# Scan drain, weight ring and FFN token sums of a hybrid encoder layer rearranged

## The chip, the cores and the metric

The kernel runs on one core of one Trainium2 chip. The metric is the device time of one execution in microseconds (us). The engines are TensorE (PE in the profile; PEld is its weight load), VectorE (DVE), ScalarE (ACT), GpSimd (POOL) and SyncE (SP), which issues the DMAs. Each engine takes its instructions in order; they meet through semaphores.

## The reference

One layer of an encoder over 1024 tokens of width 1024, in float32:

```
hn = rms_norm(x); u = hn @ w_in
y_a = MLA attention(u) @ w_br_mla      # 8 heads
y_b = forgetting attention(u) @ w_br_fox   # 8 heads
y_c = rms_norm((ssd_scan(...) + D * xh) * silu(z)) @ w_br_ssm
merged = g0 * y_a + g1 * y_b + g2 * y_c    # g = sigmoid(u_gate + b)
x = x + merged @ w_out
a = causal_dwconv(rms_norm(x) @ ffn_w_up) # 2 x 2816 columns, 3 taps
x = x + (silu(a_gate) * a_val) @ ffn_w_down
```

The scan carries a state of 16 heads, 64 by 128, from chunk to chunk; inside a chunk it is a masked product with exponentials of cumulated decays.

## The kernel before

**Products.** Every float32 product is made of three matmuls: each operand is split in a high part (rounded to the matmul's type by an ACT copy) and a low part (the rest, a DVE subtraction), and high x high, high x low and low x high are added in PSUM. `split` (L131) is the pair of instructions, `mm3` (L156) the loop. A matmul here is 128x128 by 128x512 as a rule.

**Order.** In the stages that matter PE's order is that of the program (`manual_schedule`); the instructions of the other engines are placed by a scheduler which simulates a timeline, except those wrapped in `pin`, which keep their program order. Tiles come from pools; a tag with `bufs` n is a ring of n buffers, and a tile that is laid over an older one, in its ring or in a closed pool, waits for that one's readers.

**The scan.** After the attention comes the scan over 8 chunks of 128 tokens, written as three generators. `ssd_a` transposes a chunk's inputs, forms the decay sums (`pse`, L1143, one PSUM bank with tag "seg") and their exponentials E; `ssd_b` (a chunk later) updates the state and forms the outputs (`py`, L1177, two banks with tag "py"), multiplies by the gate and scales each token by a reciprocal root (`rsqrt`, L140, all DVE, L1205 to L1208); `ssd_c` (a chunk later again) transposes the outputs (`stp`, L1216) and stores them to ys_d. `merge` interleaves these on PE with `fill`, a generator of independent projection matmuls (`all_fill`, L774; its matmuls are L791), by the share of its cost that each stream has done. Ten steps run; FILL_SSD (L1024) is how much of fill each step asks for, in units in which three matmuls are 0.65. What fill has left when the steps end is done afterwards.

**The merge and w_out.** Three branch products (`ybr`) run over 8 column tiles j and two token halves; the last branch adds up `merged[j]` and splits it to `mh`, `ml` (L1285, L1286). Then the pool of the early stages closes, a new one (`fill2`, L1290) opens in its place, w_out is loaded and split to `oh`, `ol` (L1373 to L1386), and `wo` runs over eight token tiles t and two column halves nh. `norm2` (L1302) normalises tile t-1 and transposes it (`pt`) into h2h, h2l; for the later half of the tokens it forms combinations instead, one of them T3f.

**The FFN's first matrix.** It is multiplied by a scheme with fewer products: seven block products per pair of column tiles instead of eight, with sums of weight blocks (S12, S34, `sums`, L1430) and of token blocks (T1 to T4). `prepare` (L1455) makes T3, T2 and T4 out of T3f on DVE and ACT, within the first pair. The first FIRST = 3 pairs have two of their products put ahead (`a_`, L1420). Each pair then needs products b0, c0, d0, sums X, Y, a convolution of three taps (`fa`, L1522 to L1525), silu and a product, and is stored to act_d.

**The FFN's second matrix.** It also runs as seven products (`steps`, L1536), 11 k-steps each, `dn` (L1624). The first EARLY = 3 loads use the FFN's rings; the rest use the pool "dr", which opens after "sk" (L1582, L1583).

Of the kernel before, what the change touches and what calls it, by code (L numbers as in the profile page):

```python
# [21 lines left out]
P = 128  # L22
D = 1024
# [19 lines left out]
def block_kernel(ctx: ExitStack, tc: tile.TileContext, x, positions, norm_mix_g, w_in, b_gate,  # L43
# [87 lines left out]
    def split(h, l, src, he=None, le=None):  # L131
        he = he or A
        le = le or V
        if he is A:
            A.activation(h, src, AF.Copy)  # L135
        else:
            he.tensor_copy(h, src)
        le.tensor_sub(l, src, f32(h))  # L138

    def rsqrt(pool, y, v, n):  # L140
# [6 lines left out]
        for _ in range(3):  # L147
# [6 lines left out]
            V.scalar_tensor_tensor(out=y, in0=t, scalar=1.5, in1=y, op0=ALU.add, op1=ALU.mult)  # L154

# [868 lines left out]
    FILL_SSD = [12.6] * 8 + [13.0, 13.0]  # L1024
# [45 lines left out]
    with ExitStack() as ps__:  # L1070
# [37 lines left out]
        def ssd_a(o, c):  # L1108
# [33 lines left out]
            for q in range(4):  # L1142
                pse = psp.tile([P, 512], F32, name=uid("pse"), tag="seg", bufs=1)  # L1143
# [13 lines left out]
        def ssd_b(o, c, prev):  # L1157
# [18 lines left out]
            def outputs(q):  # L1176
                py = psp.tile([P, 4, P], F32, name=uid("py"), tag="py", bufs=2)  # L1177
# [27 lines left out]
            V.tensor_scalar(v, ss, 1.0 / D, EPS, op0=ALU.mult, op1=ALU.add)  # L1205
            r = pool.tile([P, 1], F32, name=uid("yr1"), tag="yr1")
            rsqrt(pool, r, v, 1)
# [37 lines left out]
    with ExitStack() as pe_:  # L1245
        mp_ = pe_.enter_context(TP("mgp", 1))
        psp = pe_.enter_context(TP("pse", 6, space=PSUM))
        merged = [mp_.tile([P, S], F32, name=f"mg{j}", tag=f"mg{j}") for j in range(NK)]
# [4 lines left out]
        for b, wsrc, nk in ((1, w_br_fox, 4), (0, w_br_mla, 4), (2, w_br_ssm, 8)):  # L1253
# [15 lines left out]
            for j in range(NK):  # L1269
# [3 lines left out]
                for half in range(2):  # L1273
# [9 lines left out]
                    if b == 2:  # L1283
                        V.tensor_add(m, m, g[:, hs])
                        A.activation(mh[half][:, j, :], m, AF.Copy, scale=0.5)  # L1285
                        V.scalar_tensor_tensor(out=ml[half][:, j, :], in0=m, scalar=0.5,  # L1286
                                               in1=f32(mh[half][:, j, :]), op0=ALU.mult, op1=ALU.subtract)
    psg.close()
    pfl.close()
    fpl = ctx.enter_context(TP("fill2", 2, side="right"))  # L1290
# [6 lines left out]
    t3p = pt3.enter_context(TP("t3p", 1))  # L1297
    T3f = t3p.tile([P, 4, 512], F32, name="T3f", tag="T3f")
# [3 lines left out]
    def norm2(t, xt):  # L1302
        xn = fpl.tile([P, D], F32, name=uid("xn"), tag="t4", bufs=3)
# [20 lines left out]
        if half == 1:  # L1324
            b12 = xrp.tile([P, 4, P], F32, name=uid("b12"), tag="b12", bufs=2)
            A.activation(b12, pts[0], AF.Copy)
            V.tensor_sub(T3f[:, :, cs], pts[1], b12)
            e = V if t >= NT - 2 else G
            e.tensor_sub(b12, b12, f32(h2h[0][:, 0:4, cs]))
            e.tensor_sub(b12, b12, f32(h2l[0][:, 0:4, cs]))  # L1330
            hs = h2h[1][:, 0:4, cs]
            A.activation(hs, b12, AF.Copy)
            V.tensor_sub(h2l[1][:, 0:4, cs], b12, f32(hs))
# [11 lines left out]
    def halves(raw, n=NK):  # L1345
        tag, pool, bufs = ("wh", "wl"), fpl, 3
        if n == 4:
            tag, pool, bufs = ("h22", "l22"), upb, 1
        h = pool.tile([P, n, P], F32R, name=uid(tag[0]), tag=tag[0], bufs=bufs)
        l = pool.tile([P, n, P], F32R, name=uid(tag[1]), tag=tag[1], bufs=bufs)  # L1350
        split(h, l, raw)
        return h, l
# [13 lines left out]
    FIRST = 3  # L1366
# [3 lines left out]
    op_ = po_.enter_context(TP("op", 1))  # L1370
    wov = w_out[0].rearrange("(k p) c -> p k c", p=P)
    oh, ol = [], []
    for nh in range(2):  # L1373
        h = op_.tile([P, NK, 512], F32R, name=uid("woh"), tag=f"woh{nh}")
        l = op_.tile([P, NK, 512], F32R, name=uid("wol"), tag=f"wol{nh}")
        for k in range(0, NK, 2):
            late = nh == 0 and k >= 4
            raw = fpl.tile([P, 2, 512], F32, name=uid("raw"), tag="t4" if late else "wr", bufs=3 if late else 2)
            SY.dma_start(raw, wov[:, k:k + 2, 512 * nh:512 * nh + 512])
            if nh == 0:  # L1380
                for i in range(2):
# [295 lines left out]
```

## Time and profile before

| | us |
|---|---|
| median of three runs | 2154.65 |
| lowest and highest of them | 2147.74, 2155.8 |
| the profiled execution's own time | 2151.87 |
| its span | 2150.1 |
| w_out's first to last matmul | 1382.6 to 1481.8 |
| FFN first matrix, from its first product | 1483.7 to 1932.3 |
| FFN second matrix | 1932.1 to 2146.4 |

The profile shows one execution. A view of waits gives, for an engine, the line whose instruction waited, what ended the wait, and then the total, the number and the longest. A window gives the length of a stretch, the busy time of PE, PEld, DVE, ACT and POOL in it with their instructions, then the granted clock of PE as a share of full speed, the share of the DMA engines and their GB/s. A timeline row gives start, length, engine, line, operation, out<-in and shapes, and in brackets the idle time before it with its releaser. A group row ends with the total and mean (ns) of an instruction, then the idle time ahead of them. Matmuls overlap, so the mean of one is longer than their spacing.

### The profile page before, as it was taken

Reading aid. Unit: us, or ns where it says so; the run is one execution under the profiler, and the core shown is the slowest. Engines: PE = TensorE matmul, PEld = TensorE weight load, DVE = VectorE, ACT = ScalarE, POOL = GpSimd, SP = SyncE. Lnnn points to the kernel's source line nnn. Section 1 sums busy time; section 2 is a strip of 40 time slices with the busy share of each in tenths; the row PEclk is TensorE's granted clock in tenths of the full one; section 3 lists DMA queues with packets and bytes.
Section 4 is the critical chain, followed back from the end, with each engine's and each line's share of the span. In section 5 each row is a group of like instructions: output and inputs, shape, how many; then the busy total and the mean of one; then the engine's idle time right before and its main releaser. Section 6 shows DMA issues by size and latency. Waiting matters only on the chain. (4 is left out here: it accounts for less than half of the span.)

```text
span 2150.1 us, 29015 instructions
## 1 busy us (share of the span) xinstructions
PE 2056.7 (96%) x10221; PEld 1689.0 (79%) x10221; DVE 1414.1 (66%) x2574; ACT 948.2 (44%) x1701; POOL 669.9 (31%) x626
## 2 busy tenths in 40 slices
PE   7999899999999999999999799999899999999999
PEld 6898687778888888887777688777678888887887
DVE  6686478356766666657887356457887777665655
ACT  5554222145555555545555223223444444444432
POOL 2453123222222222222110030003454554431855
PEclk9999999999999999999999899999999999999999
DMA  5167667654344355424342565241122222239665
GB/s 169 36 190 217 235 208 231 207 153 127 108 135 123 104 136 137 110 76 130 109 129 94 167 200 186 98 147 50 59 88 79 79 89 79 79 111 321 239 210 196
DMA packets 275608, 303.07 MB, mean 141 GB/s; under 512 B 19292, under 2 KB 208744, under 8 KB 275464
## 3 DMA queue, kind: packets, MB, share of 16 engines
q1 hardware_dynamic: 275464, 301.24, 45.3%
q8 instruction: 80, 1.31, 0.3%
q14 instruction: 64, 0.52, 0.1%
HBM read 208.51 MB, written 92.67 MB: 140 GB/s over the span
## 5 line engine op out<-in xcount | busy, mean ns | idle before, releaser
L791 PE MATMUL mm<-hnh,wh 128*128 128x512 f32 x576 | 241.1, 419 | 1.6 <-ACT wh L741 1.6
L931 POOL TENSOR_SCALAR pm<-pm,rs 128x128 f32<-128x128 f32 (+7 forms) x128 | 108.5, 851 | 403.8 <-DVE rs L930 268.1
L791 PE MATMUL mm<-hnh,wl 128*128 128x512 f32 x576 | 228.6, 397 | 0.5 <-DVE wl L742 0.5
L791 PE MATMUL mm<-hnl,wh 128*128 128x512 f32 x576 | 228.1, 396 | 0.0
L1624 PE MATMUL dn<-dr,dr 128*128 128x512 f32 x616 | 190.8, 391 | 0.8 <-DVE dr L138 0.8
L924 ACT ACTIVATE pm<-s,nmx 128x128 f32<-128x128 f32 (+2 forms) x192 | 110.4, 580 | 71.1 <-DVE nmx L921 57.0
L1624 PEld LDWEIGHTS dn<-dr,dr 128*128 128x128 f32 x616 | 116.3, 189 | 25.1 <-DVE dr L138 1.1
L791 PEld LDWEIGHTS mm<-hnh,wl 128*128 128x128 f32 x576 | 109.1, 189 | 26.2 <-DVE wl L742 1.0
L791 PEld LDWEIGHTS mm<-hnh,wh 128*128 128x128 f32 x576 | 110.1, 191 | 20.9 <-issue 2.9
L791 PEld LDWEIGHTS mm<-hnl,wh 128*128 128x128 f32 x576 | 109.7, 190 | 17.0 <-issue 0.2
L905 PE MATMUL s<-qk,qk 96*128 96x384 f32 (+5 forms) x480 | 119.0, 352 | 3.4 <-DMA qk<-q_h 2.0
L1624 PE MATMUL dn<-dr 128*128 128x512 f32 x308 | 120.5, 391 | 1.8 <-ACT dr L135 1.8
L991 DVE TENSOR_TENSOR ptl<-tp,pth 128x512 fp32r<-128x512 f32 (+1 forms) x160 | 98.7, 632 | 29.9 <-ACT pth L990 28.9
L138 DVE TENSOR_TENSOR dr<-dr,dr 128x1024 fp32r<-128x1024 f32 x55 | 77.2, 1405 | 56.1 <-ACT dr L135 52.0
L162 PE MATMUL fx<-w5h,hnh 128*128 128x512 f32 x256 | 102.2, 404 | 7.7 <-ACT w5h L135 7.7
L135 ACT ACTIVATE wh<-wr 128x1024 fp32r<-128x1024 f32 (+1 forms) x46 | 41.9, 910 | 153.1 <-PE ybr L162 70.3
L990 ACT ACTIVATE pth<-tp 128x512 fp32r<-128x512 f32 (+1 forms) x160 | 84.1, 555 | 43.5 <-PE tp L985 43.1
L162 PE MATMUL ybr<-ah,wh 128*128 128x512 f32 x256 | 101.1, 400 | 1.6 <-ACT ah L135 1.6
L162 PE MATMUL fx<-w5h,hnl 128*128 128x512 f32 x256 | 102.3, 401 | 0.0
L162 PE MATMUL fx<-w5l,hnh 128*128 128x512 f32 x256 | 101.2, 397 | 0.0
L162 PE MATMUL ybr<-al,wh 128*128 128x512 f32 x256 | 100.9, 396 | 0.0
L162 PE MATMUL ybr<-ah,wl 128*128 128x512 f32 x256 | 100.6, 395 | 0.0
(442 smaller groups left out, 5763.1 us busy)
## 6 DMA issues: line engine op xcount, KB each, us to landing
dr<-act_d SPq DMA_DIRECT2D x99, 256.0 KB
wr<-in_ffn_w_up_dram SPq DMA_DIRECT2D x46, 512.0 KB
wr<-in_w_in_dram SPq DMA_DIRECT2D x36, 512.0 KB
g_d<-t SPq DMA_DIRECT2D x24, 512.0 KB
gl<-g_d SPq DMA_DIRECT2D x24, 512.0 KB
ws<-in_ffn_w_down_dram SPq DMA_DIRECT2D x22, 512.0 KB
wsum_d<-ws SPq DMA_DIRECT2D x22, 512.0 KB
act_d<-fa SPq DMA_DIRECT2D x22, 512.0 KB
```

Source lines behind the costliest of these rows:

```text
L135: A.activation(h, src, AF.Copy)
L138: le.tensor_sub(l, src, f32(h))
L162: T.matmul(ps, a(k), b(k), start=(i == 0), stop=(i == n - 1))
L791: T.matmul(ps, a[:, k, :], b[half][:, k, :], start=(k == 0 and i == 0), stop=(k == NK - 1 and i == 2))
L905: T.matmul(ps[:, :w], q_[:, qs], k_[:, a:a + w], start=i_ == 0, stop=not last and i_ == len(o.passes) - 1)
L924: pss[cj][1][0] = later(0.9 + 0.1 * cj, lambda cj=cj, a_=a_, b_=b_: A.activation(p_[:, a_:b_], pss[cj][0][:, :b_ - a_], AF.Exp, bias=nb, a ...
L931: G.tensor_scalar(p_[:, 0:n * P], p_[:, 0:n * P], rs[:, 3:4], 0.0, op0=ALU.mult, op1=ALU.add)
L990: later(cs + 0.05, lambda th=th, pt=pt, off=off: A.activation(th[:, :off], pt[:, :off], AF.Copy))
L991: pl[0] = later(cs + 0.6, lambda th=th, tl=tl, pt=pt, off=off: V.tensor_sub(tl[:, :off], pt[:, :off], f32(th[:, :off])))
L1624: T.matmul(ps[m], a[:, ts_], b[:, 512:], start=first_ and k == 0 and q == 0, stop=k == NFH - 1 and q == 2, skip_group_check=not first_)
```

## The change

It does the following:

- FILL_SSD goes from 12.6 in eight steps and 13.0 in two to 11.3 in eight, 12.0 and 24.5. The scan's sums `pse` and outputs `py` share one ring of three banks. The mean square and the reciprocal root of the scan's output go to POOL, except two integer instructions that stay on DVE (`rsqrt_pool`).
- The pool of the early stages stays open. The weight halves wh, wl of the FFN come from a ring of three over two pools (`whl`); "t4" has four buffers; `cv` takes its tile from it. `merged` sits in four pools of its own, and w_out's halves in five, of which four lie in their places. The first 36 matmuls of w_out take k 0 to 3 of three tiles, then k 4 to 7 follow.
- `norm2` makes T2f, T3f and T4f tile by tile, on DVE. `prepare` is replaced by `t_split`, which only splits these three, pinned.
- FIRST is 4; the copies of the early products are pinned. For the first pair the weight sums are made in place on POOL while w_out runs; for the second they are made on DVE; Y is added on DVE for two pairs. The first pair's products come in the order of the others, but for b0.
- The pool "dr" opens ahead of "sk". The last three k-steps of the last product are done output tile by output tile. The DMA scratch of the program is given as 1024.

```diff
+    def rsqrt_pool(pool, y, v):
+
+        yi = pool.tile([P, 1], I32, name=uid("rg_i"), tag="rg_i")
+        V.tensor_single_scalar(yi, v.bitcast(I32), 1, op=ALU.logical_shift_right)
+        V.tensor_scalar(y.bitcast(I32), yi, -1, RSQRT_MAGIC, op0=ALU.mult, op1=ALU.add)
+        vh = pool.tile([P, 1], F32, name=uid("rg_v"), tag="rg_v")
+        G.tensor_scalar(vh, v, -0.5, 0.0, op0=ALU.mult, op1=ALU.add)
+        for _ in range(3):
+            t = pool.tile([P, 1], F32, name=uid("rg_t"), tag="rg_t")
+            G.tensor_scalar(t, y, y, vh, op0=ALU.mult, op1=ALU.mult)
+            G.tensor_scalar(y, t, 1.5, y, op0=ALU.add, op1=ALU.mult)
...
-    FILL_SSD = [12.6] * 8 + [13.0, 13.0]
+    FILL_SSD = [11.3] * 8 + [12.0, 24.5]
...
-                pse = psp.tile([P, 512], F32, name=uid("pse"), tag="seg", bufs=1)
+                pse = psp.tile([P, 512], F32, name=uid("pse"), tag="py", bufs=3)
...
-                py = psp.tile([P, 4, P], F32, name=uid("py"), tag="py", bufs=2)
+                py = psp.tile([P, 4, P], F32, name=uid("py"), tag="py", bufs=3)
...
-            V.tensor_scalar(v, ss, 1.0 / D, EPS, op0=ALU.mult, op1=ALU.add)
+            G.tensor_scalar(v, ss, 1.0 / D, EPS, op0=ALU.mult, op1=ALU.add)
             r = pool.tile([P, 1], F32, name=uid("yr1"), tag="yr1")
-            rsqrt(pool, r, v, 1)
+            rsqrt_pool(pool, r, v)
...
+        mgs = [pe_.enter_context(TP(f"mg{i}", 1)) for i in range(4)]
...
-    pfl.close()
-    fpl = ctx.enter_context(TP("fill2", 2, side="right"))
+    fp3 = ctx.enter_context(TP("fill3", 1, side="right"))
+    turn = [0]
+
+    def whl():
+
+        turn[0] += 1
+        pool, bufs = (fp3, 1) if turn[0] % 3 == 0 else (fpl, 2)
+        return [pool.tile([P, NK, P], F32R, name=uid(n), tag=n, bufs=bufs) for n in ("wh", "wl")]
...
-            b12 = xrp.tile([P, 4, P], F32, name=uid("b12"), tag="b12", bufs=2)
-            A.activation(b12, pts[0], AF.Copy)
-            V.tensor_sub(T3f[:, :, cs], pts[1], b12)
-            e = V if t >= NT - 2 else G
-            e.tensor_sub(b12, b12, f32(h2h[0][:, 0:4, cs]))
-            e.tensor_sub(b12, b12, f32(h2l[0][:, 0:4, cs]))
+            t2 = T2f[:, :, cs]
+            A.activation(t2, pts[0], AF.Copy)
+            V.tensor_sub(T3f[:, :, cs], pts[1], t2)
+            V.tensor_sub(t2, t2, f32(h2h[0][:, 0:4, cs]))
+            V.tensor_sub(t2, t2, f32(h2l[0][:, 0:4, cs]))
             hs = h2h[1][:, 0:4, cs]
-            A.activation(hs, b12, AF.Copy)
-            V.tensor_sub(h2l[1][:, 0:4, cs], b12, f32(hs))
+            A.activation(hs, t2, AF.Copy)
+            V.tensor_sub(h2l[1][:, 0:4, cs], t2, f32(hs))
+            V.tensor_sub(t2, pts[1], t2)
+            V.tensor_sub(T4f[:, :, cs], f32(h2h[0][:, 4:8, cs]), t2)
+            V.tensor_add(T4f[:, :, cs], T4f[:, :, cs], f32(h2l[0][:, 4:8, cs]))
...
-    FIRST = 3
+    FIRST = 4
...
+    ops = [po_.enter_context(TP(f"op{i}", 1)) for i in range(5)]
...
+            h, l = (ops[4 if nh else 2 * kk + i].tile([P, 4, 512], F32R, name=uid(n), tag=f"{n}{nh}{kk}")
+                    for i, n in enumerate(("woh", "wol")))
...
+    for t in range(3):
+        wo_part(head[t], t, 0, 0, 4)
...
+                s2 = xrp.tile([P, 4, P], F32, name="s2", tag="s2")
+                G.tensor_sub(ri[:, 0:4, :], ri[:, 0:4, :], rj[:, 0:4, :])
+                G.tensor_add(rj[:, 0:4, :], rj[:, 0:4, :], rj[:, 4:8, :])
+                G.tensor_sub(s2, rj[:, 4:8, :], ri[:, 0:4, :])
+                G.tensor_sub(ri[:, 4:8, :], ri[:, 4:8, :], s2)
...
     for n in range(FIRST):
+        if n == 3:
+            first[n] = halves(first[n])
+            a_.append(bank("ua"))
+            product(a_[n], first[n], 0, *B11)
+            done_.append(upb.tile([P, S], F32, name=uid("cg"), tag="cg", bufs=FIRST))
+            pin(A.activation(done_[n][:, 512:], a_[n], AF.Copy))
         product(a_[n], first[n], 4, *B21, first=False)
-        A.activation(done_[n][:, 0:512], a_[n], AF.Copy)
+        pin(A.activation(done_[n][:, 0:512], a_[n], AF.Copy))
...
-    def prepare():
-        t = [T3f[:, k, :] for k in range(4)]
+    def t_split(t, f):
         for k in range(4):
-            split(T3[0][k], T3[1][k], t[k])
-        for k in range(4):
-            V.tensor_add(t[k], t[k], f32(B11[0][k]))
-            V.tensor_add(t[k], t[k], f32(B11[1][k]))
-            split(T2[0][k], T2[1][k], t[k])
-        for k in range(4):
-            V.tensor_sub(t[k], f32(B21[0][k]), t[k])
-            V.tensor_add(t[k], t[k], f32(B21[1][k]))
-            split(T4[0][k], T4[1][k], t[k])
+            pin(A.activation(t[0][k], f[:, k, :], AF.Copy))
+        for k in range(4):
+            pin(V.tensor_sub(t[1][k], f[:, k, :], f32(t[0][k])))
+
+    t_split(T3, T3f)
+    t_split(T2, T2f)
+    t_split(T4, T4f)
...
+            S12, S34 = sums(ri, rj, V if n == 1 else G)
...
-        cv = upa.tile([P, S], F32, name=uid("cv"), tag="cv")
+        cv = fpl.tile([P, S], F32, name=uid("cv"), tag="t4", bufs=4)
...
-        Y = tmp("Y")
-        G.tensor_add(Y, e5, e7)
-        G.tensor_add(cv[:, 512:], X, Y)
+        e = V if n < 2 else G
+        e.tensor_add(e5, e5, e7)
+        e.tensor_add(cv[:, 512:], X, e5)
...
+    dr[0] = ctx.enter_context(TP("dr", 1))
     sp[0] = ctx.enter_context(TP("sk", 1))
-    dr[0] = ctx.enter_context(TP("dr", 1))
...
+            if pi == len(steps) - 1 and NFH - LAST <= k:
+                if k < NFH - 1:
+                    continue
+                todo = [(m, j) for m in range(4) for j in range(NFH - LAST, NFH)]
```

## What was predicted

> **What bounds the kernel now.** I read the page's first part, then the waits of TensorE (PE), then the windows around each long wait, and only then the chain.
>
> ```profile
> span 2150.1 us, 29015 instructions
> PE 2056.7 (96%) x10221; PEld 1689.0 (79%) x10221; DVE 1414.1 (66%) x2574; ACT 948.2 (44%) x1701; POOL 669.9 (31%) x626
> ```
>
> PE is busy 96% of the span, and the change leaves the number of matmuls as it is (it reorders some). So what can be gained is the other 4%, 93 us, and the time in which PE runs at a lower granted clock. The waits of PE, each with its total, its count and its longest:
>
> ```profile
> PE stp L1216 <- ACT y L1208: 9.8, 1, 9.8
> PE pse L1144 <- ACT E L1149: 4.8, 7, 1.0
> PE ub L1359 <- DVE cbl L138: 4.0, 4, 2.0
> PE ud L1359 <- DVE cbl L138: 3.8, 2, 2.3
> PE uc L1359 <- ACT e L1495: 3.0, 3, 1.4
> PE wo L162 <- ACT woh L135: 2.7, 1, 2.7
> PE ua L1359 <- ACT cg L1481: 2.5, 1, 2.5
> PE pt L1318 <- DVE xn L1310: 2.5, 2, 1.5
> PE dn L1624 <- ACT dr L135: 1.8, 1, 1.8
> PE dn L1624 <- DVE dr L138: 0.8, 1, 0.8
> ```
>
> These are the waits in the stages that the diff touches: 35.7 us. The rest of the 93 us lies in stages ahead of the scan, which the diff leaves alone. The windows place them (length, then busy time of PE, PEld, DVE, ACT, POOL, then granted clock):
>
> ```profile
> 955.00:1180.00 225.00, 219.41 (x1063) 165.88 (x1061) 172.91 (x301) 122.44 (x198) 41.00 (x16) 0.98 0.38 115
> 1180.00:1200.00 20.00, 7.86 (x44) 6.32 (x44) 5.56 (x17) 7.29 (x11) 0.00 (x0) 0.74 0.38 125
> 1200.00:1210.00 10.00, 10.00 (x38) 8.00 (x38) 5.15 (x6) 2.78 (x4) 0.00 (x0) 0.85 0.76 249
> 1380.00:1388.00 8.00, 4.92 (x13) 3.70 (x14) 6.92 (x11) 4.90 (x9) 0.00 (x0) 0.79 0.60 208
> 1498.00:1530.00 32.00, 23.50 (x86) 16.60 (x85) 30.89 (x39) 15.01 (x22) 15.59 (x6) 0.89 0.06 17
> 1550.00:1577.00 27.00, 21.85 (x91) 16.54 (x90) 22.54 (x18) 11.85 (x15) 18.20 (x11) 1.00 0.29 97
> 1926.00:1945.00 19.00, 16.46 (x65) 12.87 (x64) 12.06 (x12) 8.72 (x9) 2.59 (x2) 0.91 0.75 252
> ```
>
> The reader is to see two things. Each hole in PE is short and has its own cause: the drain of the scan has nothing on VectorE (DVE) or ScalarE (ACT) either, a pure chain, while in 1498 to 1530 DVE is busy 30.89 of 32 us, a true bound. And after a hole the clock is down: 0.85 over 1200 to 1210 is 1.5 us lost at full PE occupation, 0.79 over 8 us is 1.7 us, 0.89 over 32 us is 3.5 us, 0.91 over 19 us is 1.7 us. A hole that goes takes this with it.
>
> **The scan.** Before, FILL_SSD asks for 12.6 units of projection matmuls (fill) in each of eight steps and 13.0 in each of the last two. Rows for what comes of it, and for the reciprocal root that is moved to GpSimd (POOL):
>
> ```profile
> L791 PE MATMUL mm<-hnh,wl x184: 388/393/632, 954.7 to 1183.6; 128*128 128x512 f32 x184
> 1190.68 1.06 ACT L1203 ACTIVATE yT<-y 128x1024 f32<-128x1024 f32 x1 [4.79 <-DMA ys_d<-yT]
> L150 DVE SCALAR_TENSOR_TENSOR rs_t<-yr,rs_v 128x1 f32<-128x1 f32 x17 | 10.2, 603 | 0.3
> L154 DVE SCALAR_TENSOR_TENSOR yr<-rs_t,yr 128x1 f32<-128x1 f32 x17 | 9.4, 555 | 0.5
> L226 POOL TENSOR_SCALAR rt<-rt 128x128 f32<-128x128 f32 x32 | 9.6, 301 | 2.4
> L931 POOL TENSOR_SCALAR pm<-pm,rs 128x128 f32<-128x128 f32 x16 | 9.3, 580 | 36.0 <-DVE rs L930 34.7 <-PE s L918 1.4
> L1137 POOL TENSOR_TENSOR xdd<-xT,dend 128x1024 f32<-128x1024 f32 x7 | 19.8, 2822 | 138.8 <-ACT xT L1118 138.8
> L1139 POOL TENSOR_TENSOR y<-xT,Db 128x1024 f32<-128x1024 f32 x8 | 19.6, 2456 | 0.0
> 1578.91 2.75 PE ud L1359 x12
> ```
>
> The last fill matmul starts at 1183.6, before the 9.8 us wait: the tenth step asked for 13.0 and got nothing, since the fill had run out. So the new 24.5 for that step isn't what it gets either. It gets what the others no longer take: 8 x (12.6 - 11.3) + (13.0 - 12.0) = 11.4 units; 0.65 units are three matmuls, so 53, in yields of 12 some 48. Twelve matmuls of this size take 2.75 us (the last row, from the chain), 0.23 each, so 11 us of work now stand where PE waited. The chain that they must cover was 9.8 us. It loses part of its wait for the ys_d store (4.79 us of it), because the transposes of the step before come earlier against its end, and eight of its DVE instructions are now POOL ones. A POOL instruction on [128,1] isn't in the trace: below, 0.1 us less than the 0.3 us of the 128x128 form with constants; above, the 0.58 us of the form with a column from memory, next to a working DVE. I take 0.3, as nearest in an idle drain: 8 x 0.3 = 2.4 us plus the hand-overs to DVE and back; at 0.58 it would be 4.6. Covered either way. The wait goes (9.5), and of the clock after it 1.5: **11 us**. What is late next is the second group of transposes and the first ybr, both behind ACT; I leave both as they are.
>
> Inside the scan PE is idle 225 - 219.4 = 5.6 us, of which 4.8 are pse waiting for the one bank of the sums. Three banks in rotation with py remove that, as a bank comes round only after two others. Steps get shorter by 1.3 / 0.65 x 3 x 0.23 = 1.4 us, so DVE must do its share in less time; but six of its [128,1] instructions, 3 x (603 + 555) = 3.5 us a chunk, leave it. **4 us** (ends: -2 and 9, with the 0.98 clock of this window regained).
>
> [...]
>
> **The start of w_out.** wo waits 2.7 us for the first split of w_out; in the window of 8 us PE is idle 3.1 us in all and loses 1.7 us by the clock: 4.8. Now w_out's halves sit in four pools laid over four pools of the merged sum, so that the first eight k-halves need only columns long finished, and the first 36 matmuls (8.3 us) need only k 0 to 3. ACT and DVE have room for these splits under the last ybr products, PE being full there. **4 us**; nothing if the order written for ACT still puts them behind the last merge.
>
> **norm2.** T2f, T3f and T4f are now made tile by tile in norm2, on DVE: five more 128x512 instructions for t = 4, 5 and three more for t = 6, 7, 16 in all. What one takes, and rows for the next part:
>
> ```profile
> 1507.81 0.68 DVE L1461 TENSOR_TENSOR T3f<-T3f,hnl 128x512 f32<-128x512 f32 x1
> 1492.30 0.87 PE pt L1318 x8
> 1550.21 3.90 DMA wr<-in_ffn_w_up_dram
> 1554.25 1.53 POOL S L1432
> 1558.31 1.07 ACT wh L135
> L1525 DVE SCALAR_TENSOR_TENSOR fa<-cg,pc_f,fa 128x1023 f32<-128x1023 f32 (+1 forms) x44 | 57.7, 1311 | 1.5 <-ACT fa L1522 1.4
> L1529 DVE TENSOR_TENSOR fa<-fa,fa 128x1024 f32<-128x1024 f32 x22 | 40.0, 1818 | 0.3
> ```
>
> One takes 0.68 us (the first row), so 16 x 0.68 = 10.9 us on DVE, spread over four tiles of 11 us of matmuls (48 x 0.23). They lie beside PE; the two pt waits (2.5) stay, and I charge **2 us more** (ends 0 and 6).
>
> **From norm2 to the FFN.** This is the largest term. Between the last transposes (they end at 1493.2) and the end of the fourth pair of FFN columns (the ud row of 1578.91, to 1581.7) PE does 36 + 24 + 4 x 60 = 300 matmuls, 69 us at 0.23, in 88.5 us: 19.5 us too long. The waits of ub, ud, uc and ua are 13.3 of it, the clock 3.5. The cause in 1498 to 1530 is prepare(): 12 ACT copies and 28 DVE instructions ahead of the products with T3, T2 and T4. Sixteen of the 28 move into norm2, and a fourth pair's first product (24 matmuls, 5.5 us) is put ahead of them. What remains, 12 x 0.68 = 8.2 us on DVE, fits in the 14 us from the last transposes to the first product that needs it. Against this, four pairs instead of three now have only 60 matmuls (14 us) on PE. In each DVE has fa 4 x 1.3, the product 1.8, three sums of 0.7, splits 3.4: 12.5 of 14 us, and the second pair also gets four sums from POOL (2.7). And a loop runs through h22, which has one buffer: last product of pair n, split 1.3, load 3.9, POOL sums 4.1 (1554.25 to the split at 1558.31), splits 2.4, first product of pair n + 2: 11.7 us at the least and some 16 behind a full DVE queue, against 14 of PE. I let 1 us stay at T3 and 2 us at each of three pairs: 7 of 19. **12 us** (ends: 3 and 19).
>
> **From the FFN to its second matrix.** PE waits 1.8 + 0.8 and loses 1.7 of clock.
>
> ```profile
> 1921.21 10.61 SPq L1566 DMA_DIRECT2D sk<-wsum_d  x9
> 1932.34 0.43 SPq L1566 DMA_DIRECT2D dr<-in_ffn_w_down_dram  x1
> 1938.45 1.06 ACT L135 ACTIVATE dr<-dr 128x1024 fp32r<-128x1024 f32 x1 [2.56 <-DMA dr<-in_ffn_w_down_dram]
> 2144.42 2.73 DVE L1646 TENSOR_TENSOR x<-dn,dX 128x512 f32<-128x512 f32 x4 [8.72 <-PE dn L1624]
> 2145.14 2.37 SPq L1600 DMA_DIRECT2D out_dram<-x  x4
> ```
>
> The sync queue issues nine sk loads, each when its place comes free, over 10.6 us, and the dr load that PE needs first stands behind them at 1932.3. The change swaps the places of the two pools, so that sk's come free last and dr's first; the queue's order should follow. **3 us** of 4.3 (ends 0 and 4.3). The tail gets the last three k-steps grouped by output tile, but the last tile's sum and store still follow the last matmul (the last two rows): 0.
>
> **The sum.** 11 + 4 + 4 - 2 + 12 + 3 = 32 us off the profiled execution's 2151.87 us: 2120 us. That execution is 2.8 below the median of the three runs (2154.65; 2147.74 to 2155.8), within their spread. A measurement of this kernel can tell a difference of about 0.5% (10.8 us) from no change.
>
> **Rivals.** (1) The early FFN pairs are bound by the loop through h22 and DVE: 5 us a pair are then lost at three pairs, and the 12 us are 3: 2129, up to 2138 if the scan's 4 and the down start's 3 fail too. For it speaks 12.5 of 14 us on DVE; against it, DVE loses prepare(). (2) All that the waits show goes: 19 + 9.8 + 1.5 + 5.6 + 4.8 + 4.3 = 45: 2107. (3) It doesn't do what it says: ACT's and DVE's order still puts w_out's splits and the T splits late, and only the drain is won: 11 us less some pair waits of 5, 2146. (4) Slower: a new wait in the scan. The moved root has DVE wait for POOL's first instruction, with everything behind it in DVE's queue: the products E by cbm, the El splits, the y sums, and so py on PE. If POOL is then inside xdd and y (L1137 and L1139, 2.8 + 2.5 us), each of eight chunks stops for up to 5.3 us: 42 us against the 28 that the other places give, 2166. It decides from 3.5 us a chunk. Against it: POOL is idle 139 of the 175 us in its row. [...]
>
> **How the numbers follow.** Forecast (2108 to 2127) 0.55; rival 1, 0.2; rival 2, 0.1; rival 3, 0.09; rival 4, 0.06. The range takes in forecast, rivals 1 and 2 and the ends of the unknown terms: 2103 to 2143, leaving out about 0.15 to 0.2. Faster by over 0.5%: 0.86; within: 0.08; slower: 0.06.
>
> **What would show it.** In the profile of the changed kernel: no stp wait on y over 2 us, and fill matmuls up to the scan's end; no pse wait; a granted clock of 1.0 where w_out starts; PE's share above 97%; under 8 us of waits of ub, uc, ud, ua together, and those on wl or e rather than cbl; dr loads issued ahead of sk's. The prediction is wrong if ACT's y of the last chunk comes more than 12 us after the last py, if pairs two to four take 18 us each, or if DVE's integer shift in the scan waits for POOL.

## The result, and the profile after

The changed kernel takes 2118.06 us (median of four runs, 2114.19 to 2119.88); the kernel before took 2153.55 beside it (2147.74 to 2155.8). The ratio is 0.9837 with a 95% interval of 0.9812 to 0.9862. The profiled execution after took 2116.97 us, 34.9 less than the profiled one before. The forecast was 2120.

First the page's first part, after:

```profile
span 2115.3 us, 28991 instructions
PE 2046.9 (97%) x10221; PEld 1686.4 (80%) x10221; DVE 1385.9 (66%) x2519; ACT 944.2 (45%) x1702; POOL 670.1 (32%) x678
```

PE has as many matmuls as before and is busy 9.8 us less with them (the clock for the most part, 0.992 over the span instead of 0.986; w_out's matmuls also follow each other faster, see below), and the span is 34.8 shorter: the other 25 us were idle time. The view of PE's waits after, for the stages that the diff touches (total, count, longest):

```profile
PE uc L1379 <- ACT e L1548: 3.0, 2, 2.8
PE ua L1379 <- ACT cg L1526: 2.5, 1, 2.5
PE dn L1680 <- ACT wh L134: 2.3, 1, 2.3
PE ub L1379 <- DVE wl L135: 1.6, 3, 0.6
PE stp L1225 <- ACT y L1217: 1.1, 2, 0.8
PE dn L1680 <- DVE wl L135: 0.8, 1, 0.8
```

The waits of pse on E in the scan (4.8), of wo (2.7), of pt in norm2 (2.5) and on cbl (4.0 and 3.8) are gone, and that on y fell from 9.8 to 1.1. One has grown: uc now waits 2.8 us in one piece for a copy e (1.4 at most before). The cg wait and those of dn are as long as they were.

To see where the 34.8 us came from, I cut the two spans at the same matmuls (first and last of each name in PE's timeline):

| stage | before | after | gain | forecast |
|---|---|---|---|---|
| up to the attention's last product | 964.4 | 961.6 | 2.8 | 0 |
| scan, to the first ybr | 235.2 | 219.2 | 16.0 | 15 |
| ybr, to the first wo | 183.0 | 180.3 | 2.7 | 4 for both of these |
| w_out and norm2, to the last pt | 110.6 | 102.9 | 7.7 | and -2 for norm2 |
| to the end of the FFN's fourth pair | 88.5 | 75.4 | 13.1 | 12 |
| the rest of the FFN's first matrix | 350.6 | 357.5 | -6.9 | 0 |
| its second matrix | 214.1 | 214.6 | -0.5 | 3 |
| what follows | 3.7 | 3.7 | 0 | 0 |

The windows of the kernel before for the scan and for w_out with norm2 (length, busy PE, PEld, DVE, ACT, POOL, clock, DMA share, GB/s):

```profile
964.40:1199.60 235.20, 217.62 (x1047) 163.82 (x1046) 175.81 (x314) 127.28 (x205) 41.00 (x16) 0.96 0.38 118
1382.60:1493.20 110.60, 107.63 (x485) 86.58 (x486) 67.50 (x140) 31.64 (x52) 10.22 (x8) 0.98 0.41 133
```

and after:

```profile
961.60:1180.80 219.20, 212.09 (x1048) 160.90 (x1046) 157.64 (x250) 124.84 (x205) 64.66 (x80) 1.00 0.40 124
1361.00:1464.00 103.00, 103.00 (x487) 85.53 (x486) 66.37 (x151) 28.28 (x46) 5.12 (x4) 1.00 0.36 118
```

In the scan PE was idle 17.6 us before and is idle 7.1 after; another 5.5 of the 16.0 us are PE's shorter busy time, with the clock at 1.00 instead of 0.96. PE is without a hole through all of w_out and norm2.

Most kernels below were run once, so these are the bounds for reading single executions. Nine of the kernels measured here have the same scan; their scans take 219.1 to 223.7 us. And ahead of the scan, where all kernels are alike, they take 961.4 to 966.9. So a difference of a stage under some 5 us in the scan is not evidence by itself, and the 2.8 us of the first row are nothing that the change did. Behind the scan, in kernels that have there what the changed kernel has, the stretch from the first ybr to the first wo takes 179.9 to 182.1 us (twelve kernels), w_out with norm2 102.9 to 103.0, the time from the last pt to the end of the fourth pair 75.4 to 77.1 and to the end of the FFN's first matrix 432.9 to 434.4 (seven kernels), and the second matrix 212.3 to 214.6 (ten). For the fourth pair the changed kernel's own 75.4 is the lowest of these. I therefore compare stages and waits, not whole times, except where a ratio is given.

### The profile page after: what moved, and what is told of

Same layout as the page of the kernel before. It is cut to its first block, busy times and chain, and to the rows that moved or that the text cites. A ratio compares the mean times of both kernels' runs of the same rounds, so it can differ in the third digit from the quotient of the medians.

```text
span 2115.3 us, 28991 instructions
## 1 busy us (share of the span) xinstructions
PE 2046.9 (97%) x10221; PEld 1686.4 (80%) x10221; DVE 1385.9 (66%) x2519; ACT 944.2 (45%) x1702; POOL 670.1 (32%) x678
## 4 chain that ended last, share of the span: by engine, by line
PE 69%; ACT 3%; DVE 2%; POOL 2%; DMA 2%; issue 1%; SPq 0%; ACTq 0%; POOLq 0%; DVEq 0%
PE mm L800 16%; PE dn L1680 10%; PE ybr L171 9%; PE ua L1379 5%; PE uc L1379 5%; PE ud L1379 4%; PE wo L1424 4%; PE s L914 4%; PE tp L994 2%; PE ub L1379 2%; PE o L959 1%; PE o L967 1%; ACT pm L933 1%; DMA wr<-in_ffn_w_up_dram 1%; PE py L1190 1%
## 5 line engine op out<-in xcount | busy, mean ns | idle before, releaser
L800 PE MATMUL mm<-hnl,wh 128*128 128x512 f32 x576 | 227.2, 395 | 0.0
L1680 PE MATMUL dn<-dr,dr 128*128 128x512 f32 x592 | 182.4, 389 | 0.0
L1680 PEld LDWEIGHTS dn<-dr,dr 128*128 128x128 f32 x592 | 111.1, 188 | 23.2
L1680 PE MATMUL dn<-dr 128*128 128x512 f32 x296 | 115.2, 389 | 0.0
L1475 POOL TENSOR_TENSOR S<-wr 128x512 f32<-128x512 f32 x20 | 26.8, 1341 | 268.2 <-DMA wr<-in_ffn_w_up_dram 237.0
L135 DVE TENSOR_TENSOR dr<-dr,dr 128x1024 fp32r<-128x1024 f32 x52 | 72.8, 1401 | 53.0 <-ACT dr L134 44.0
L171 PE MATMUL fx<-w5h,hnh 128*128 128x512 f32 x256 | 102.7, 406 | 3.5 <-ACT w5h L134 3.5
L171 PE MATMUL fx<-w5h,hnl 128*128 128x512 f32 x256 | 102.7, 403 | 0.0
```

The lines of the kernel that those rows point to most:

```text
L135: return i, le.tensor_sub(l, src, f32(h))
L171: T.matmul(ps, a(k), b(k), start=(i == 0), stop=(i == n - 1))
L800: T.matmul(ps, a[:, k, :], b[half][:, k, :], start=(k == 0 and i == 0), stop=(k == NK - 1 and i == 2))
L1680: T.matmul(ps[m], a[:, ts_], b[:, 512:], start=first_ and j == 0 and q == 0, stop=j == NFH - 1 and q == 2, skip_group_check=not first_)
```

## The experiments

Each kernel is the changed one with one edit, unless it says otherwise. The edits are given as they differ from the changed kernel.

### The scan: fill, banks, root

**The fill back as it was.**

```diff
-    FILL_SSD = [11.3] * 8 + [12.0, 24.5]
+    FILL_SSD = [12.6] * 8 + [13.0, 13.0]
```

> The changed kernel with FILL_SSD as before ([12.6] * 8 + [13.0, 13.0]), all else changed. Theory (fill kept for the drain covers it): the stp wait on y returns at 9 to 10 us with half a clock window behind it, and the stretch from the last attention matmul to the first ybr grows from 219 to about 229 us. Rival (the drain got short because of the banks and the earlier store): the wait stays under 4 us and the stretch under 223.

**The banks back as they were.**

```diff
-   pse = psp.tile([P, 512], F32, name=uid("pse"), tag="py", bufs=3)
+   pse = psp.tile([P, 512], F32, name=uid("pse"), tag="seg", bufs=1)
...
-   py = psp.tile([P, 4, P], F32, name=uid("py"), tag="py", bufs=3)
+   py = psp.tile([P, 4, P], F32, name=uid("py"), tag="py", bufs=2)
```

> The changed kernel with pse in one bank of its own and py in two, as before. Theory: pse waits for ACT's E again, 4 to 5 us in all, and the stretch from the last attention matmul to the first ybr is 223 to 225 instead of 219. Rival (the waits came from a full DVE, which the moved root empties): pse waits under 2 us and the stretch within 1 us of 219.

**Both of these edits.**

> Both the fill list and the three scan banks are put back as before the change; the root on POOL, the token sums in norm2 and everything behind the scan stay as after. Theory (the scan's steps and its drain share one amount of idle time, so the two edits are worth something only together): the scan takes 234 to 237 us as in the kernel before (235.2), because with the long fill in the steps the wait of the scan sums for ACT's exponentials falls back from 9.3 to about 4.8 us, and the 11 us wait on y behind the last step returns; whole run about 2133 to 2137 us by the profile. Rival (the two costs measured singly, 8.0 and 16.6 us, add to 219.2): a scan of 243 to 245 us, with a 9 us wait of the scan sums as well as the 11 us wait on y; whole run about 2142 us.

The wait rows and the scan's window of the three. Fill as before:

```profile
PE stp L1225 <- ACT y L1217: 11.0, 1, 11.0
```

```profile
963.60:1190.80 227.20, 213.05 (x1047) 161.14 (x1045) 157.18 (x250) 125.80 (x205) 65.19 (x80) 0.97 0.40 122
```

Banks as before:

```profile
PE pse L1153 <- ACT E L1158: 9.3, 11, 1.6
PE stp L1225 <- ACT y L1217: 0.8, 1, 0.8
```

```profile
963.90:1199.70 235.80, 220.37 (x1047) 166.03 (x1046) 156.13 (x250) 127.30 (x205) 65.99 (x80) 0.97 0.38 115
```

Fill and banks as before:

```profile
PE stp L1225 <- ACT y L1217: 11.0, 1, 11.0
PE pse L1153 <- ACT E L1158: 6.1, 10, 0.9
```

```profile
965.50:1203.60 238.10, 217.89 (x1047) 163.60 (x1045) 157.72 (x250) 126.78 (x205) 65.31 (x80) 0.96 0.38 117
```

The reader can lay the scans out as a square. With the new banks the scan takes 219.2 us (new fill) and 227.2 (old fill); with the old banks 235.8 and 238.1.

- The fill is worth 8.0 us beside the new banks and 2.3 beside the old ones, which is within the scatter. Beside the old ones it does take away the 11.0 us wait on y, but the steps, now with less fill, wait 9.3 instead of 6.1 us for E, and PE is busy 2.5 us longer (220.4 against 217.9, at a clock of 0.97 and 0.96).
- The banks are worth 10.9 us beside the old fill and 16.6 beside the new one. The expectation of 4 to 6 us, which was the prediction's 4, was far too small: the wait on E is 4.8 us in the kernel before, but with the old banks PE is also busy longer for the same matmuls, at a lower granted clock (0.97 against 1.00 beside the new fill, 0.96 against 0.97 beside the old one). Beside the new fill it is idle 8.3 us longer (15.4 against 7.1) and busy 8.3 us longer (220.4 against 212.1); beside the old fill it is 6.1 and 4.8.
- The last kernel was to tell a shared gain (234 to 237 us) from two that add up (243 to 245). It took 238.1, beyond the first range by 1.1 and short of the other by 5. The wait on E fell back as the theory has it, to 6.1, not to 4.8. So the two edits overlap, by some 6 us here; with a scatter of 5 us in this stage the size of the overlap is not settled. The whole run took 2140.16 us, above the theory's 2133 to 2137 and near the rival's 2142, but 3.9 us of it arose ahead of the scan.

**The root back on DVE.**

```diff
-   G.tensor_scalar(v, ss, 1.0 / D, EPS, op0=ALU.mult, op1=ALU.add)
+   V.tensor_scalar(v, ss, 1.0 / D, EPS, op0=ALU.mult, op1=ALU.add)
...
-   rsqrt_pool(pool, r, v)
+   rsqrt(pool, r, v, 1)
```

> The changed kernel with the scan's mean square and reciprocal root on DVE as before. Theory (the root was a load on DVE in each step): 2 to 4 us longer from the last attention matmul to the first ybr, as stp, py and pse waits inside the steps; in the drain the chain gets about 1 us shorter (POOL's eight took 3.1 us, DVE's 1.9). Rival (the steps have room for it): within 1 us of 219, or shorter.

The scan took 218.7 us, against 219.1 to 223.7 with the root on POOL: the theory's 2 to 4 us aren't there. POOL's root brings nothing that can be seen here, and costs nothing. Where it stands uncovered it is the slower one. In the drain after, POOL's timeline has its first and last instruction at

```profile
1172.58 0.19 POOL L1214 TENSOR_SCALAR yv<-yss 128x1 f32<-128x1 f32 x1 [16.27 <-ACT yT L1212]
...
1175.39 0.26 POOL L163 TENSOR_SCALAR yr<-rg_t,yr 128x1 f32<-128x1 f32 x1
```

which is 3.1 us, and DVE's in the drain before

```profile
1191.86 0.15 DVE L1205 TENSOR_SCALAR yv<-yss 128x1 f32<-128x1 f32 x1 [4.71 <-ACT yT L1203]
...
1193.58 0.16 DVE L154 SCALAR_TENSOR_TENSOR yr<-rs_t,yr 128x1 f32<-128x1 f32 x1
```

which is 1.9. The wait on y shows that 1.2 us: 9.8 before, 11.0 with the old fill and the root on POOL.

### The start of w_out

**w_out's halves in one pool**, each half one tile of eight k, with the order of the first 36 matmuls kept:

```diff
-    ops = [po_.enter_context(TP(f"op{i}", 1)) for i in range(5)]
+    op_ = po_.enter_context(TP("op", 1))
...
+        h = op_.tile([P, NK, 512], F32R, name=uid("woh"), tag=f"woh{nh}")
+        l = op_.tile([P, NK, 512], F32R, name=uid("wol"), tag=f"wol{nh}")
```

> The changed kernel with w_out's halves in one pool and in tiles of eight k, as before; the order k 0 to 3 first stays. Theory (the finer pools let the first splits run under the last ybr products): the first wo matmul waits 2 to 3 us for woh or wol again and a half-speed clock window follows; last ybr to last pt 3 to 5 us longer than 102.9. If the spacing of the wo matmuls (0.235 us before, 0.229 now) hangs on the tiles' shape and place, it goes back and adds some 2 us more. Rival (order of k alone does it): 102 to 104, spacing 0.229.

Its waits, and windows at the start of w_out and within it:

```profile
PE wo L1419 <- ACT woh L134: 2.7, 1, 2.7
PE wo L1419 <- DVE wol L135: 0.5, 1, 0.5
```

```profile
1370.40:1373.80 3.40, 3.40 (x11) 2.67 (x10) 3.40 (x6) 1.95 (x4) 0.00 (x0) 0.57 0.79 254
1395.00:1440.00 45.00, 44.96 (x216) 37.25 (x214) 26.74 (x72) 10.79 (x20) 1.20 (x1) 1.00 0.44 139
```

Both waits of before are back to the tenth, and behind them 3.4 us at 0.57 of the clock: 3.3 us more ahead of the first wo and 2.6 behind it. So the five pools, with their tiles of four k, are what hides w_out's splits, and not the order of the first 36 matmuls alone; pools and tile size were not undone apart. A second question got the answer no. In a stretch of 45 us well inside w_out, PE ran 209 matmuls before,

```profile
1422.00:1467.00 45.00, 45.00 (x209) 36.60 (x207) 26.04 (x63) 11.19 (x19) 2.58 (x2) 1.00 0.32 105
```

and 216 here, as after. The count overstates it, since five to seven more of these are short transposes of norm2 (25 before, 30 after, 32 here). But from the start of one wo matmul to the next the median is 234 ns before, and 227 after and here, at a clock of 1.00. What makes w_out's matmuls follow each other faster is therefore not the shape of its tiles. It stays open.

### From norm2 to the FFN

**The token sums behind norm2**, where prepare had them: 12 DVE instructions leave norm2, and 16 do their work between the splits.

```diff
-            V.tensor_sub(t2, pts[1], t2)
-            V.tensor_sub(T4f[:, :, cs], f32(h2h[0][:, 4:8, cs]), t2)
-            V.tensor_add(T4f[:, :, cs], T4f[:, :, cs], f32(h2l[0][:, 4:8, cs]))
...
+    for k in range(4):
+        V.tensor_add(T2f[:, k, :], T3f[:, k, :], f32(B11[0][k]))
+        V.tensor_add(T2f[:, k, :], T2f[:, k, :], f32(B11[1][k]))
     t_split(T2, T2f)
+    for k in range(4):
+        V.tensor_sub(T4f[:, k, :], f32(B21[0][k]), T2f[:, k, :])
+        V.tensor_add(T4f[:, k, :], T4f[:, k, :], f32(B21[1][k]))
```

> The changed kernel with the sums for T2 and T4 made after norm2 in 16 DVE instructions, as prepare did, and not tile by tile in norm2. Theory: they stand in front of the products again, 16 x 0.62 = 10 us of DVE, of which the head start of the fourth pair hides a part: from the last pt to the end of the first ordinary pair 106 to 111 us instead of 100.6; the stretch of w_out and norm2 stays at 103 or gets 0 to 1 us shorter. Rival 1 (the fourth pair's head start covers it): 101 to 103. Rival 2 (the loop of loads and POOL sums paces the pairs, and it runs on meanwhile): under 103 as well, but with the waits of ub and ua in the later pairs gone.

**Three pairs put ahead**, as before the change.

```diff
-    FIRST = 4
+    FIRST = 3
```

> The changed kernel with FIRST = 3, so that the fourth pair's products aren't put ahead. Theory (the wait of ua on cg belongs to the first pair that isn't early, wherever that is; the head start covers the T splits): the wait of 2.5 us on cg moves one pair ahead, the wait for T grows by some 3 us, and the time from the last pt to the end of pair index 4 is 102 to 105 instead of 100.6. Rival (the fourth early pair gives back what it wins): 99 to 101.

**Both of these edits.**

> The changed kernel with both undone: the sums for T2 and T4 after norm2, and FIRST = 3. Alone they left the time from the last pt to the end of pair index 3 at 75.2 and 79.6, against 75.4. Theory (each covers for the other: the DVE sums hide under the fourth head start, or they aren't there): together 84 to 89, close to the 88.5 of the kernel before, with waits of ub and ud on cbl of 5 us or more. Rival (another part of the change brought the gain, the weight sums on POOL and DVE or the order of the products): 79 to 82.

Time from the last pt to the end of a pair, us:

| | fourth pair | fifth pair | end of the first matrix |
|---|---|---|---|
| before | 88.5 | 108.0 | 439.1 |
| after | 75.4 | 100.6 | 432.9 |
| token sums late | 75.2 | 102.7 | 434.5 |
| three pairs ahead | 79.6 | 99.1 | 431.0 |
| both | 84.9 | 104.4 | 436.2 |

The expectations for the first two named the fifth pair. The token sums late came out in rival 1's range (102.7 against 101 to 103) and not in the theory's, and three pairs ahead at the rival's end (99.1 against 99 to 101). Both together fell in the theory's range (84.9 against 84 to 89 at the fourth pair).

With both undone waits on cbl come back, if less than the 5 us expected, and the cg wait is at the fourth pair:

```profile
PE ud L1376 <- DVE cbl L1504: 4.3, 4, 3.0
PE ua L1376 <- ACT cg L1529: 3.0, 1, 3.0
```

With the sums alone late, hardly any of it is left:

```profile
PE ud L1376 <- DVE cbl L1504: 1.4, 1, 1.4
PE ub L1376 <- DVE wl L135: 2.6, 3, 1.6
```

Each of the two edits covers for the other: together they are worth 9.5 us at the fourth pair (84.9 to 75.4), but the sums alone bring 5.3 (84.9 to 79.6) and the head start alone 9.7 (84.9 to 75.2). At the end of the first matrix the picture turns: there the sums alone bring 5.2 us (436.2 to 431.0), both 3.3, and the head start alone 1.7, which is about what executions of the same code differ by. So with the sums in norm2 the fourth pair's head start costs 1.9 to 3.4 us by the end of the first matrix (431.0 against 432.9 to 434.4). It moves the cg wait one pair on and doesn't remove it. This is why the changed kernel's gain of 13.1 us at the fourth pair is 7.4 at the fifth: the window that the prediction chose ends between the two places of that wait. And w_out with norm2 took 102.9 us with those 12 instructions, 103.0 without: they cost nothing. With both undone 84.9 is still 3.6 less than the 88.5 before; the rest of the change (the weight sums on POOL and DVE, the order of the products, the rings) wasn't undone, so what brings these 3.6 is not shown.

The new wait has its cause in ACT's timeline after:

```profile
1478.94 0.60 ACT L1496 ACTIVATE cg<-ua 128x512 f32<-128x512 f32 x1 [3.14 <-PE ua L1379]
1479.43 2.18 ACT L1505 ACTIVATE cbh<-T3f 128x512 fp32r<-128x512 f32 x4
1481.52 2.19 ACT L1505 ACTIVATE cbh<-T2f 128x512 fp32r<-128x512 f32 x4
1483.60 2.18 ACT L1505 ACTIVATE cbh<-T4f 128x512 fp32r<-128x512 f32 x4
1485.68 1.04 ACT L134 ACTIVATE wh<-S 128x1024 fp32r<-128x1024 f32 x1
1486.63 0.58 ACT L1548 ACTIVATE e<-uc 128x512 f32<-128x512 f32 x1
```

The pinned copies of T3, T2 and T4 run twelve in a row, and the copy e that empties a bank for PE stands behind the last of them.

**That copy ahead of T2's split.** The splits of T2 and T4 move into the first pair, behind its e.

```diff
     t_split(T3, T3f)
-    t_split(T2, T2f)
-    t_split(T4, T4f)
...
         A.activation(e5, c0_, AF.Copy)
+        if n == 0:
+            t_split(T2, T2f)
+            t_split(T4, T4f)
```

> The changed kernel with the splits of T2 and T4 pinned behind the copy e5 of the first pair instead of ahead of it. Theory (uc's wait of 2.8 us is ACT's order: twelve pinned copies stand ahead of e5): that wait falls under 0.7. From the last pt to the end of pair index 4 the time then falls by 2 to 3 us if nothing else paces the pairs, and by less than 1 if the loop through h22, its load and POOL's sums does, the waits of ub on wl growing by as much. I hold the second the likelier.

```profile
PE uc L1379 <- ACT e L1546: 0.2, 1, 0.2
```

The wait goes, and with it 3.1 us at the fourth pair (72.3) and 2.9 at the end of the first matrix (430.0), against the changed kernel's profile, the fastest of the seven at both places. I had held it likelier that another wait would take its place; none did.

### From the first to the second matrix

SP's timeline after, where the loads of the second matrix begin:

```profile
1884.94 0.32 SPq L1577 DMA_DIRECT2D act_d<-fa  x1
1896.72 0.32 SPq L1645 DMA_DIRECT2D x<-x_d  x1
1897.09 0.42 SPq L1615 DMA_DIRECT2D dr<-act_d  x1
1897.56 0.43 SPq L1616 DMA_DIRECT2D dr<-in_ffn_w_down_dram  x1
```

The sk loads no longer stand ahead of the dr loads. But the queue issues nothing for 11.8 us, since its head is now another load, of the residual x, that waits for its place, which comes free only with the last products of the first matrix. SP's own waits after show it:

```profile
SPq L1645 <- PE ud L1379: 11.7, 1, 11.7
```

**The residual's load in program order**, so behind the weights:

```diff
-        SY.dma_start(t, x2_d[4 * r + m, :, 512 * c:512 * c + 512])
+        tc.keep_in_program_order(SY.dma_start(t, x2_d[4 * r + m, :, 512 * c:512 * c + 512]))
```

> The changed kernel with the residual loads (x from x_d) kept behind the loads that the program issues ahead of them, in the sync queue. Theory (the queue's head, a residual load whose place comes free only with the last product, holds back the loads of the second matrix from 1884.9 to 1896.7): the dn waits of 2.4 + 0.8 us and the clock window after them go, 4 to 5 us less from the end of ud to the end of dn. Rival (these loads wait for their own places or for bandwidth): 0 to 1 us.

```profile
1889.22 0.32 SPq L1577 DMA_DIRECT2D act_d<-fa  x1
1892.01 0.32 SPq L1615 DMA_DIRECT2D dr<-act_d  x1
1892.39 0.42 SPq L1616 DMA_DIRECT2D dr<-in_ffn_w_down_dram  x1
```

The first dr load is issued 2.8 us behind the last store. The second matrix takes 210.6 us instead of 214.6, and 210.5 and 210.6 in the two kernels below that have this edit too, against 212.3 to 214.6 without it: 1.7 to 4.1 us are gained, where the theory had 4 to 5. The dn wait of 2.3 us is gone, that of 0.8 on wl is 0.7.

### The two repairs together

> The changed kernel with both repairs, the residual loads behind the others and e5 ahead of the splits of T2 and T4. Theory (two separate places, their gains add): last pt to the end of ud 430 instead of 433, ud to the end of dn 210.6 instead of 214.6; 6 to 7 us under the changed kernel, 2111 to 2112. Rival (what is won is lost at the first ordinary pair or by the clock): 2115 to 2118.

2112.91 us (median of four, 2109.53 to 2116.26) beside 2155.23 for the kernel before: a ratio of 0.9806, interval 0.9788 to 0.9824. The median lies between the theory's range and the rival's, nearer to the theory's. The stages show both: 430.2 us to the end of the first matrix, 210.5 for the second. Against the changed kernel's 0.9837 the intervals overlap, so that it is faster than that one rests on these two stages rather than on the ratios: 6.8 us against that profile, and 4.5 against the fastest of the kernels that have the changed kernel's code in each.

What PE still waits for at the start of the FFN is the cg wait. **Y of the fourth pair on DVE** as well, on top of both repairs, was to free POOL for the sums ahead of cg:

```diff
-        e = V if n < 2 else G
+        e = V if n < 2 or n == 3 else G
```

> The same with Y of pair index 3 also added on DVE. Theory (the wait of ua on cg, 2.5 us, is ACT's copy behind fa of cv, which waits for POOL's sum): the wait falls under 1 and the time to the end of pair index 4 by 1 to 3 us. Rival (DVE is as late as POOL): no change against e5_and_residual.

```profile
PE ub L1379 <- DVE wl L135: 3.8, 3, 2.7
PE uc L1379 <- ACT e L1546: 2.2, 1, 2.2
```

The cg wait is gone, so POOL's sum was what it waited for. These two waits, most of them in the fifth pair, stand in its place. Where DVE adds Y as well, it is likely to be late with the weight halves; no run shows that apart. The fifth pair ends 100.7 us after the last pt, 3.0 later than with the two repairs alone; the ratio is 0.9824 (0.9804 to 0.9844).

## Why the prediction was right, and where not

The sum was right: 32 us were forecast and 34.8 came in the profiles, 2.8 of them ahead of the scan, where the change does nothing. Its terms were less right than their sum, so that a part of the agreement is luck.

**The scan (15, measured 16.0).** The drain's mechanism held. Of the fill's matmuls after (duration in ns, first and last start),

```profile
L800 PE MATMUL mm<-hnh,wl x184: 388/393/404, 951.9 to 1175.7; 128*128 128x512 f32 x184
```

the last starts 5.1 us ahead of the first ybr, and the wait on y is 0.8 at its longest. But the chain that the fill covers did not get shorter, as was forecast. A sign of being wrong, ACT's y more than 12 us after the last py, did come: 14.1 us after (the last py ends at 1161.6), where it was 9.1 before.

```profile
1164.31 0.60 PE L1225 MATMUL stp<-ident,y 128*128 128x128 f32 x4
1166.40 0.86 SPq L1228 DMA_DIRECT2D ys_d<-yT  x1
1175.68 1.15 ACT L1217 ACTIVATE y<-y,yr 128x1024 f32<-128x1024 f32 x1 [3.19 <-POOL yr L163]
```

The kept fill stands ahead of the second group of transposes as well: they start 2.7 us after the last py instead of at once, and the ys_d store behind them 4.8 us after it instead of 1.2 (1185.92 before). The longer chain is covered all the same, because some 60 matmuls of fill run behind the last py (14.3 us of busy PE) where the prediction counted 48 (11 us).

And as two terms, 11 and 4, the step failed. It priced the banks by the wait that they remove (4.8) and by a clock put at nearly nothing; they measured 10.9 to 16.6, of which 4.8 to 8.3 is longer busy time of PE at a lower clock (0.96 and 0.97, where the new banks have 0.97 and 1.00), beyond the upper end of 9. And it added the two as if they were separate: the fill is worth 8.0 only with the banks there. That less DVE work by the moved root would help was wrong: 0. Of rival 4 the wait itself came, and was named as a sign of being wrong: DVE's integer shift waits 9.8 us in the scan for POOL's first instruction, in three places, 7.2 of it in the drain. But with the root on DVE its first instruction there waits 9.8 us for ACT, and the scan takes the same: the wait wasn't new and cost nothing.

POOL's chain has long instructions beside DVE's. Its first kind in the scan, after, minimum, median and maximum in ns:

```profile
L162 POOL TENSOR_SCALAR rg_t<-yr,rg_v x24: 337/341/1858, 1005.5 to 1174.9; 128x1 f32<-128x1 f32 x24
```

The longest is 1.9 us instead of 0.34. What makes it long is not shown: no run isolates it, and the timelines only say what ran beside it. The prediction's 603 ns is a mean of two kinds: in the scan before, 40 of the root's 48 DVE instructions on two tensors take 0.15 to 0.22 us, and eight take 1.8 to 1.9. Each of the eight starts while POOL is inside xdd or y, and ends within 0.1 us of the end of POOL's instruction:

```profile
1042.03 2.41 POOL L1137 TENSOR_TENSOR xdd<-xT,dend 128x1024 f32<-128x1024 f32 x1 [20.62 <-ACT xT L1118]
1042.59 1.86 DVE L150 SCALAR_TENSOR_TENSOR rs_t<-yr,rs_v 128x1 f32<-128x1 f32 x1
```

After, eight of POOL's 48 take 0.6 to 1.9 us, each beside a two-tensor instruction of DVE. None of this is seen in the stage's time: with the root on either engine it takes the same (218.7 us on DVE, 219.1 to 223.7 on POOL).

**The start of w_out and norm2 (4 and -2, measured 2.7 and 7.7).** The start held: with the pools undone 5.9 us come back, where 4.9 had been lost (waits of 2.7 and 0.5, and 1.7 by the clock, 0.79 over 8 us). What norm2 would cost was forecast with the wrong sign. The two pt waits of 2.5 us went instead of staying (what removed them wasn't tried apart), and the 12 DVE instructions that were moved back cost nothing. That leaves 10.4 less 4.9 (the waits and the clock at the start) less 2.5, some 3 us, for matmuls that follow each other faster (384 of them, 7 ns closer by the median). The prediction had no term for this, and its cause is open.

**From norm2 to the FFN (12, measured 13.1 in the window named).** Of the 19.5 us lost, 6.4 are left (75.4 against 69), where 7 were forecast. The waits of ub, uc, ud and ua are 8.1 us instead of the 13.3 of before, and on e, cg and wl, not on cbl, as was said; the sign named was under 8. But the cause was put too simply: not the sums and the head start together, but either of them takes away most of the waits on cbl that are there with both undone. And the window was too short. Behind it 6.9 us are given back, so that the first matrix in all gains 6.2: the cg wait stands at the fifth pair instead of the fourth, and that pair takes 25.2 us instead of 19.5, with 3.4 us of waits and one stretch of the lower clock (0.50 over 3.4 us, 1550.40 to 1553.80). Rival 1, the loop through h22, doesn't show: its waits on wl are 1.6 us, and pairs two to four take 13.9 to 14.9 us each.

**The second matrix (3, measured -0.5).** This step failed, and at the sentence "the queue's order should follow". The sk loads did move behind the dr loads, but the prediction didn't ask what else sits in SP's queue. The residual's load became its head. With that load pinned behind the others 1.7 to 4.1 us are gained, which is about what the step had meant to gain.

**The tail (0)** held.

Of the general signs, PE's share is 96.8% (2046.9 of 2115.3), not above 97, and the clock where w_out starts is 1.00.

So 32 came out near 34.8 by errors that cancelled: 8.4 us too little for w_out and norm2 and 3.8 for what lies ahead of them stood against 5.8 too much for the FFN's first matrix and 3.5 for its second.

## What to carry to other kernels

Price a removed wait by the stage with and without it, not by its row: in the scan the old banks' waits on E (9.3 and 6.1 us, the longest 1.6) came with PE busy 8.3 and 4.8 us longer, at a clock of 0.97 and 0.96 instead of 1.00 and 0.97; and two edits that fill the same idle time can't be added. End the window of a forecast behind the next regular step, not ahead of it, or a wait that only moves is counted as gone. Where an order of DMAs is changed, list everything in that queue and ask which of it will stand at the head waiting for a place.

## What was not expected of the hardware

The clock falls to about half for stretches of some 3.4 us or twice that: 0.51 over 3.4 us at w_out before (1383.90 to 1387.30), 0.50 over 3.4 us in the fifth pair after, 0.52 over 6.8 us in the row below. Around the scan's drain before it is 0.50 over 13.6 us (1189.30 to 1202.90). It does so behind short idle times too. A hole of 2.7 us at w_out is followed by one such stretch (the 0.57 row above). In the scan of the kernel with the late token sums, which there is the same as after,

```profile
997.60:1001.00 3.40, 2.95 (x20) 2.29 (x18) 2.63 (x6) 1.77 (x4) 0.00 (x0) 1.00 0.00 1
1001.00:1007.80 6.80, 6.80 (x20) 5.04 (x20) 4.30 (x8) 3.67 (x6) 0.00 (x0) 0.52 0.42 116
```

a stretch with 0.45 us of idle time is followed by 6.8 us at half the clock, with PE busy throughout. After, PE has the same hole of 0.45 us at the same place (1000.51 here, 997.88 after) and the whole scan ran at 1.00, so the hole alone doesn't bring the fall about; what tips it is open. Such a stretch is most of the scatter of 219.1 to 223.7 us in the scan: the three longest of the nine scans (222.1, 222.2 and 223.7) have a half-clock stretch of 6.8 us at this place, and the six others (219.1 to 219.7) have none there.
